# An ordering edge that keeps the products of the remaining modulation columns behind the first S5 projection on TensorE

## The chip, the core and the metric

The kernel runs on one core of a Trainium2 chip. The metric is the device time of one launch in microseconds, here the median of three runs. The program uses TensorE (matmuls), VectorE, ScalarE and GpSimd, and SyncE's queue for most of its loads and stores.

## What is computed: the reference

One layer of a diffusion backbone for 512 tokens of 1024 features, with 256 context tokens. In the reference, cut to what matters here:

```python
mod_x = (jax.nn.silu(c) @ w_ada[l] + b_ada[l])[:, None, :]
shx1, scx1, gx1, shx2, scx2, gx2 = jnp.split(mod_x, N_MOD, axis=-1)
px = modulate(rmsnorm(x, g_norm1[l]), shx1, scx1) @ w_in[l] + b_in[l]
pc = modulate(rmsnorm(ctx, g_norm1[l]), shc1, scc1) @ w_in[l] + b_in[l]
...
st_c = s5_states(uc, lam_bar, b_bar, None, dr == 1)
st_x = s5_states(ux, lam_bar, b_bar, h0, dr == 1)
y_x = y_x + s5_readout(st_x, s5_c_re[l, dr], s5_c_im[l, dr])
...
z_x = hyena_mixer(px[..., S5_W:], hy_conv_w[l], hy_conv_b[l], filt_x, hy_d[l], rows)
mix_x = merge_head_groups(y_x.reshape(B, L, S5_W), z_x, w_glu[l], b_glu[l],
...
x = x + gx1 * mix_x
hx2 = modulate(rmsnorm(x, g_norm2[l]), shx2, scx2)
x = x + gx2 * peer(hx2.reshape(B * L, D), peer_wq[l], peer_k1[l], peer_k2[l],
...
return rmsnorm(x, g_final)
```

The first projection `px` needs only the shift and the scale of the first norm (`shx1`, `scx1`), a third of the 6144 modulation columns. The other two thirds (`gx1`, `shx2`, `scx2`, `gx2`) are needed after the mixers.

## The kernel before

The front of the program, to about 476 us, computes everything up to the queries of the expert stage; behind it come the top-16 searches, the gathers and the two large products with the expert tables, which take the rest of the span. The names of the front are these.

- `pf`, `pke`, `pko`, `kk`: the Hyena filters and their spectra. A spectrum `kk` goes to the DRAM tile `KD` and comes back later as `sp`.
- `pmod`, `modr`: the first third of the modulation columns, and its transposes `modrT`, from which VectorE makes `mod` and `ax`.
- `pmodr`: the remaining columns, in two halves (`pmodr0`, `pmodr1`) of 8 steps each. A step is a call of `more_modulation`: for 128 rows of the weights two loads of 512 KB (`wb0_0_0`, `wb0_0_1`: half, step, side), and the products of each, which are four records in the trace. A "block" below is one such load with its products. The calls stand in `s5_context` and in the Hyena part, but their instructions carry a priority, so that the scheduler may draw them far forward.
- `xT0` to `xT7`: transposes of the normed input, eight blocks of 128 features. VectorE reads each out of PSUM (`xt`), and ScalarE and VectorE make the two parts `xs` (high and low) that a projection in three products needs. `cT`, `ct`, `cs` are the same for the context.
- `px0` to `px3`, `pc0` to `pc3`: the S5 part of the projection (24 matmuls each) of the tokens and of the context, with the weights `win0` to `win3`; `px4` to `px15` are the Hyena part. `px`, `pc`, `xT`, `cT` and the later `pu`, `pw` share a PSUM pool of two buffers.
- `wt1w`, `wt2w`, `et`, `E`, `ct13`, `Cr`, `ru`, `VP`, `H`: steps of the S5 scans on VectorE, in six groups; `edge`, `wt`, `pv` are their products on TensorE.
- `x2t`, `hq`: the short convolution of the Hyena part. `pu00` and `pw00` are the first products of its long convolution (with the table `fwd`), which VectorE multiplies with the spectrum in `spt000` to `spt003`.

The order in which this is written is the string `SEQ` (`M` makes `modrT`, `X` the `xT`, `U0` `px0`, `u0` `pc0`). The order in which each engine's queue holds it is made from that by a list scheduler with its own timeline, priorities and the edges that the program adds by hand (`add_manual_dep` with `NOSYNC`: it fixes an order on one engine, without a semaphore). Each engine, SyncE's queue included, then works in that order.

The weight loads share three buffers (`NRAW`, tag `wraw`): `win0r`, `win1r`, the `wb` and `win2r` onward take turns. A load is issued when the buffer's last reader is done.

Of the kernel before, what the change touches and what calls it, by code (L numbers as in the profile page):

```python
# [9 lines left out]
F32 = mybir.dt.float32  # L10
F32R = mybir.dt.float32r
# [62 lines left out]
SG = 32  # L74
# [35 lines left out]
NOSYNC = mybir.DependencyInfo(mybir.DependencyClass.NoSync, mybir.DependencyReason.DATA)  # L110
# [118 lines left out]
def build(tc, I, out, dbg=None, stop=None):  # L229
    nc = tc.nc  # L230
# [63 lines left out]
    def sm(name, shape, dtype=F32, bufs=1, tag=None):  # L294
        return cur[0].tile(shape, dtype, tag=tag or name, name=name, bufs=bufs)
# [80 lines left out]
    for what in EARLY.split():  # L376
        n = int(what[1:] or 0)
# [41 lines left out]
    sc = cp.tile([P, 8, 2], F32, tag="sc", name="sc")  # L419
# [200 lines left out]
        return s, c  # L620


    rest = [0, None]

    def more_modulation():
        with prio(PR_M):
# [2 lines left out]
    def more_modulation_():  # L629
        h_, k = rest[0] // 8, rest[0] % 8  # L630
        rest[0] += 1
        if k == 0:
            rest[1] = psn(f"pmodr{h_}")
            V.memset(rest[1], 0.0)
        pm = rest[1]
        for e in range(2):
            wa = wp.tile([P, D], F32, tag="wraw", name=f"wb{h_}_{k}_{e}", bufs=NRAW)
            c0 = 2048 * (h_ + 1) + D * e
            nc.sync.dma_start(wa, I["w_ada"][k * P:(k + 1) * P, c0:c0 + D])
            for n in (2 * e, 2 * e + 1):  # L640
# [39 lines left out]
    for part in SEQ.split():  # L680
        n_ = int(part[1:] or 0)
        if part[0] == "H":
            hid = feats
            for i in range(3):
                ph = ps5(f"ph{i}")[:, 0:256]
                n = 33 if i == 0 else 64
# [30 lines left out]
        elif part[0] == "S":  # L717
            t0, t1 = ((0, 4), None, (4, 6))[n_]
# [21 lines left out]
        elif part[0] == "P":  # L740
            k = n_
            if k == 0:
                pm = psm("pmod")
                V.memset(pm, 0.0)
            columns_of(pm, was[k], k, 2)
            if NWARM:
# [5 lines left out]
                for i in range(NWARM):  # L752
                    mm = PE.matmul(pwarm, warm[:, 0:P], warm, start=True, stop=True)
# [507 lines left out]
    for co in range(4):  # L1261
# [11 lines left out]
        t = g2_(f"cat5{co}", [P, 512])  # L1273
# [222 lines left out]
    def columns(lt, eid, gt):  # L1496

        ei = sm(f"ei{lt}", [P, 2, P], I32, tag="ei", bufs=2)
        V.tensor_copy(ei[:, 0], eid)
        V.tensor_scalar(ei[:, 1], ei[:, 0], 127, None, ALU.bitwise_and)  # L1500
        V.tensor_scalar(ei[:, 0], ei[:, 0], 7, None, ALU.logical_shift_right)
        ef = sm(f"ef{lt}", [P, 2, P], tag="ef", bufs=2)
        V.tensor_copy(ef, ei)
        ptr = ps.tile([P, 512], F32, tag="psc", name=f"ptr{lt}", bufs=2 if RGATE else 3)[:, 0:3 * P].rearrange("p (e n) -> p e n", e=3)
        PE.transpose(ptr[:, 0], ef[:, 0], ident)
        PE.transpose(ptr[:, 1], ef[:, 1], ident)
        PE.transpose(ptr[:, 2], gt, ident)
        if RGATE:
            t = sm(f"cols{lt}", [P, P], tag="cols", bufs=3)
            A.activation(t, ptr[:, 1], AF.Copy)  # L1510
            gh_ = sm(f"colg{lt}", [P, P], F32R, tag="colg", bufs=3)
            A.activation(gh_, ptr[:, 2], AF.Copy)
            V.tensor_tensor(ptr[:, 2], ptr[:, 2], gh_.bitcast(F32), ALU.subtract)
            return t, gh_.bitcast(F32), ptr
        t = sm(f"cols{lt}", [P, 5, P], tag="cols", bufs=3)
        A.activation(t[:, 0:3], ptr, AF.Copy)
        A.activation(t[:, 3:5], ptr[:, 0:3:2], AF.Copy, scale=-1.0)
        return t

    def gates_r(b_, cols, c0):  # L1520

        i2, gh_, ptr = cols
        st = sm(f"gst{b_}", [P, P, SG], tag="gst", bufs=2)

        def per_token(x, t0):
            return x[:, t0:t0 + 4].unsqueeze(2).broadcast_to((P, 4, P))

        for q in range(SG // 4):
            pg = ps.tile([P, 4, 2, P], F32, tag="pgg", name=f"pgg{b_}_{q}", bufs=2)
            t0 = c0 + 4 * q  # L1530
            o2 = sm(f"o2_{b_}_{q}", [P, 4, P], F32R, tag="o2", bufs=NOO)
            o1 = sm(f"o1_{b_}_{q}", [P, 4, P], tag="o1", bufs=NOO)
            os_ = sm(f"os{b_}_{q}", [P, 4, 2, P], F32R, tag="os", bufs=NOO)
            keys_ = iotak.unsqueeze(1).broadcast_to((P, 4, P))
            GP.tensor_tensor(o2, keys_, per_token(i2, t0), ALU.is_equal)
            V.tensor_tensor(o1, keys_, per_token(ptr[:, 0], t0), ALU.is_equal)
            V.tensor_tensor(os_[:, :, 1], o1, per_token(ptr[:, 2], t0), ALU.mult)
            for e in range(4):
                A.activation(os_[:, e, 0], o1[:, e], AF.Copy, scale=gh_[:, t0 + e:t0 + e + 1])
            for e in range(4):  # L1540
                mm = PE.matmul(pg[:, e].rearrange("p h i -> p (h i)"), o2[:, e], os_[:, e].rearrange("p h i -> p (h i)"), start=True, stop=True)
            groups.append(mm)
            so = st[:, :, 4 * q:4 * q + 4]
            A.activation(so, pg[:, :, 0].rearrange("p t i -> p i t"), AF.Copy)
            last = V.tensor_tensor(so, pg[:, :, 1].rearrange("p t i -> p i t"), so, ALU.add)
            gathers(G_SHARE, last)
            run_ahead(RG)
        nc.scalar.dma_start(GD[b_], st)
# [157 lines left out]
```

## Time and profile before

| | |
|---|---|
| median of three runs | 1786.19 us (1784.98 to 1787.14) |
| the profiled execution, its own time | 1782.07 us |
| its span, from the first to the last instruction | 1780.3 us |
| mean granted TensorE clock | 0.978 of full speed |
| busy, of the span | TensorE 1670.0 us (94%), VectorE 1491.0 us (84%), ScalarE 817.9 us (46%) |
| from 476 to 1778 us | TensorE busy 1264.76 of 1302 us |

All rows below come from the profiled execution, which was 4.1 us shorter than the median. Its span is 1.8 us shorter than its time. A row of a timeline gives the start in us from the span's start and the duration; a matmul's end overlaps its successor a little, so the starts tell the pace. `L441` is a line of the kernel before.

### The profile page before, as it was taken

To read this page: it belongs to the slowest core of one execution; us is meant where nothing else is said; L and a number is where in the kernel's file an instruction comes from. 1 tells how busy PE (TensorE), PEld (TensorE's weight loads), DVE (VectorE), ACT (ScalarE), POOL (GpSimd) and SP (SyncE) were. 2 spreads that over 40 slices of the span, in tenths; PEclk is the share of its full clock that TensorE was granted. 3 is DMA by queue.
4 is the path that set the end of the run, shared out by engine and by line. 5 is a ranking of instruction groups with operands and counts; after the bars stand their busy time and mean duration, and the time that the engine had idled before them with its cause. 6 is when DMAs were issued, how large, how long until landed. Compare 5 with 4: busy or idle time off the path is not lost.

```text
span 1780.3 us, 24942 instructions
## 1 busy us (share of the span) xinstructions
PE 1670.0 (94%) x8731; PEld 1410.6 (79%) x8731; DVE 1491.0 (84%) x3039; ACT 817.9 (46%) x1616; POOL 169.5 (10%) x158
## 2 busy tenths in 40 slices
PE   5799998789899999998999989999999999999997
PEld 1477654456799999998999978877878788999996
DVE  7965989986688989989999958788878787888887
ACT  3443543234433323236989844444434344444444
POOL 0000000000000000001101101111111112222221
PEclk9899999899899999999999989999999999999999
DMA  9436453122444444446989899999999998999981
GB/s 372 155 98 209 156 170 91 51 75 71 124 156 139 141 147 151 145 147 246 330 319 333 322 321 387 385 356 378 363 353 358 357 339 320 342 327 349 335 311 71
DMA packets 170228, 436.13 MB, mean 245 GB/s; under 512 B 17139, under 2 KB 102004, under 8 KB 150902
## 3 DMA queue, kind: packets, MB, share of 16 engines
q1 hardware_dynamic: 128854, 251.28, 41.8%
q0 software_dynamic: 18432, 134.23, 20.5%
q10 hardware_dynamic: 22816, 49.03, 7.6%
q8 instruction: 69, 1.13, 0.3%
q14 instruction: 57, 0.47, 0.1%
HBM read 381.52 MB, written 52.92 MB: 244 GB/s over the span
## 4 chain that ended last, share of the span: by engine, by line
PE 63%; DVE 12%; issue 1%; ACT 1%; DMA 1%; ACTq 0%; DVEq 0%
PE pacc L308 9%; PE pacc L309 9%; PE pacc L307 9%; PE pa L309 7%; PE pa L307 7%; PE pa L308 7%; PE pgg L1566 5%; PE pq L309 2%; PE pq L307 2%; PE pq L308 2%; DVE idx L1352 1%; DVE rs L1350 1%; PE pg L1266 1%; DVE idx L1348 1%; PE po L307 1%
## 5 line engine op out<-in xcount | busy, mean ns | idle before, releaser
L308 PE MATMUL pacc<-vl,wwh 128*128 128x512 f32 x768 | 299.6, 391 | 1.8 <-DVE vl L1607 1.8
L309 PE MATMUL pacc<-vh,wwl 128*128 128x512 f32 x768 | 295.1, 390 | 0.0
L1430 POOL DMA_INDIRECT uvr<-in_uv_dram,gidx x128 | 157.1, 1228 | 1090.6 <-DVE accg L1439 764.6
L307 PE MATMUL pacc<-vh,wwh 128*128 128x512 f32 x768 | 238.3, 391 | 8.4 <-ACT vh L1606 8.4
L1607 DVE TENSOR_TENSOR vl<-vr,vh 128x1024 fp32r<-128x1024 f32 x128 | 155.3, 1219 | 26.8 <-ACT vh L1606 26.7
L307 PEld LDWEIGHTS pacc<-vh,wwh 128*128 128x128 f32 x768 | 143.5, 188 | 39.4 <-ACT vh L1606 11.3
L308 PEld LDWEIGHTS pacc<-vl,wwh 128*128 128x128 f32 x768 | 144.1, 188 | 33.6 <-DVE vl L1607 3.6
L309 PEld LDWEIGHTS pacc<-vh,wwl 128*128 128x128 f32 x768 | 144.2, 188 | 29.7
L1439 DVE SCALAR_TENSOR_TENSOR accg<-uvr,wgt,accg 128x1024 f32<-128x1024 f32 x128 | 163.7, 1279 | 4.1 <-ACT wgt L1436 1.8
L1431 DVE SCALAR_TENSOR_TENSOR junk<-uvr,hrow 128x1024 f32<-128x1024 f32 x128 | 155.9, 1218 | 0.0
L1606 ACT ACTIVATE vh<-vr 128x1024 fp32r<-128x1024 f32 x128 | 133.0, 1050 | 44.1 <-PE pacc L309 33.8
L1615 ACT ACTIVATE wwh<-gw 128x384 fp32r<-128x384 f32 x128 | 67.1, 524 | 185.4 <-PE pacc L308 146.1
L1616 DVE TENSOR_TENSOR wwl<-gw,wwh 128x384 fp32r<-128x384 f32 x128 | 70.9, 554 | 53.9 <-ACT wwh L1615 53.9
L1566 PE MATMUL pgg<-o,o 128*128 128x128 f32 x768 | 93.0, 278 | 4.3 <-ACT o L1562 4.3
L1566 PEld LDWEIGHTS pgg<-o,o 128*128 128x128 f32 x768 | 92.1, 194 | 4.5 <-ACT o L1562 4.5
L1557 DVE TENSOR_TENSOR o<-iotak,cols 128x512 f32<-128x512 f32 x96 | 65.8, 685 | 10.1 <-PE pgg L1566 10.1
L1564 DVE TENSOR_SCALAR o<-iotak,cols 128x128 f32<-128x128 f32 x240 | 70.1, 342 | 0.0
L1434 ACT ACTIVATE wgt<-dots 128x1 f32<-128x1 f32 x128 | 25.3, 198 | 93.1 <-DVE junk L1431 93.1
L1562 ACT ACTIVATE o<-o,cols 128x128 f32<-128x128 f32 x144 | 63.6, 493 | 0.0
L1369 ACT ACTIVATE ga<-pa 128x384 f32<-128x384 f32 x128 | 60.4, 472 | 2.4 <-DVE gw L1612 2.1
L1568 ACT ACTIVATE gst<-pgg 128x512 f32<-128x512 f32 x96 | 56.7, 591 | 1.2 <-PE pgg L1566 1.1
L1612 DVE TENSOR_TENSOR gw<-gal,gc 128x384 f32<-128x384 f32 x88 | 48.4, 553 | 7.4 <-DMA gal<-GA 5.5
(1812 smaller groups left out, 4133.9 us busy)
## 6 DMA issues: line engine op xcount, KB each, us to landing
vr<-in_uv_dram SPq DMA_DIRECT2D x128, 512.0 KB
GD<-gst ACTq DMA_DIRECT2D x12, 2048.0 KB
gc<-GD SPq DMA_DIRECT2D x32, 768.0 KB
GA<-ga ACTq DMA_DIRECT2D x88, 192.0 KB
gal<-GA SPq DMA_DIRECT2D x88, 192.0 KB
wb<-in_w_ada_dram SPq DMA_DIRECT2D x32, 512.0 KB
wa<-in_w_ada_dram SPq DMA_DIRECT2D x8, 1024.0 KB
KD<-kk SPq DMA_DIRECT2D x16, 256.0 KB
```

What stands on the lines that cost most here:

```text
L307: nc.tensor.matmul(o, a[0], b[0], start=start, stop=False)
L308: nc.tensor.matmul(o, a[0], b[1], start=False, stop=False)
L309: nc.tensor.matmul(o, a[1], b[0], start=False, stop=stop_)
L1430: GP.indirect_dma_start(out=uvr, out_offset=None, in_=I["uv"], in_offset=bass.IndirectOffsetOnAxis(ap=gidx[:, s:s + 1], axis=0))
L1431: ins = V.scalar_tensor_tensor(junk, uvr[:, 0:D], 1.0, hrow, ALU.mult, ALU.mult, accum_out=dots[:, s:s + 1])
L1439: V.scalar_tensor_tensor(accg, uvr[:, D:2 * D], wgt[:, s:s + 1], accg, ALU.mult, ALU.add)
L1564: last = V.tensor_scalar(o1[:, e], iotak, cols[:, 0, t:t + 1], cols[:, 2, t:t + 1], ALU.is_equal, ALU.mult)
L1566: mm = PE.matmul(pg[:, e, :], o2[:, e], o1[:, e], start=True, stop=True)
L1606: A.activation(vh, vr, AF.Copy)
L1607: (V if QUIET or i >= P - VLV else GP).tensor_tensor(vl, vr, vh.bitcast(F32), ALU.subtract)
L1615: A.activation(wh, gw, AF.Copy)
L1616: last = V.tensor_tensor(wl, gw, wh.bitcast(F32), ALU.subtract)
```

## The change

A third entry of the list `rest` holds the name of the last instruction of `px0` once that is written. The next call of `more_modulation` then ties its first matmul to it by an edge without a semaphore, and clears the entry. All later products of `pmodr` follow that one. Before, nothing tied them. The other edits (the functions `columns` and `gates_r` and the loop that calls them) stand under `RGATE`, which is 0 in both programs, so that the built programs don't contain them; the diff shows the part that is built.

```diff
@@ -620,7 +620,7 @@
         return s, c
 
 
-    rest = [0, None]
+    rest = [0, None, None]
 
     def more_modulation():
         with prio(PR_M):
@@ -638,7 +638,10 @@
             c0 = 2048 * (h_ + 1) + D * e
             nc.sync.dma_start(wa, I["w_ada"][k * P:(k + 1) * P, c0:c0 + D])
             for n in (2 * e, 2 * e + 1):
-                PE.matmul(pm[32 * n:32 * n + 1], sc[:, k, 0:1], wa[:, (n % 2) * 512:(n % 2 + 1) * 512], start=k == 0, stop=k == 7, tile_position=(0, 32 * n))
+                mm = PE.matmul(pm[32 * n:32 * n + 1], sc[:, k, 0:1], wa[:, (n % 2) * 512:(n % 2 + 1) * 512], start=k == 0, stop=k == 7, tile_position=(0, 32 * n))
+                if rest[2] is not None:
+                    tc.add_manual_dep(mm.ins, rest[2], NOSYNC, reason="leaves the way to the first projections")
+                    rest[2] = None
         if k == 7:
             ptv = turned(pm, f"modr{h_}")
             for n in range(4):
@@ -657,6 +660,8 @@
         px = psa(f"px{ct}")
         for k in range(8):
             mm3(px, (wh[:, k, :], wl[:, k, :]), (xhi[k], xlo[k]), k == 0, k == 7)
+        if ct == 0:
+            rest[2] = nc.cur_bb.bb.instructions[-1].name
         if ct % 2 == 0:
             u2 = hy(f"uP{ct}", [P, 2, T8, NK])
         A.activation(u2[:, ct % 2, :, NKC:NK].rearrange("p j k -> p k j"), px.rearrange("p (k j) -> p k j", j=T8), AF.Identity, bias=b_in[:, ct:ct + 1])
@@ -1506,12 +1511,10 @@
```

The scheduler makes a new order of the whole front from it; from the queries of the expert stage on the rows are the same. Three places follow.

TensorE behind the transposes of the modulation rows (`modrT`), before:

```order
L434 MATMUL modrT_395<-ident_60,modr_393 128x98 x4
L641 MATMUL pmodr0_980<-wb0_0_0_982,sc_138 1x512 x2
L641 MATMUL pmodr0_980<-wb0_0_1_986,sc_138 1x512 x2
L641 MATMUL pmodr0_980<-wb0_1_0_1024,sc_138 1x512 x2
L641 MATMUL pmodr0_980<-wb0_1_1_1028,sc_138 1x512 x2
L441 MATMUL xT2_434<-ident_60,xrow0_99 128x128 x2
L441 MATMUL xT2_434<-ident_60,xrow2_100 128x128 x2
```

and after:

```order
L434 MATMUL modrT_395<-ident_60,modr_393 128x98 x4
L441 MATMUL xT2_434<-ident_60,xrow0_99 128x128 x2
L441 MATMUL xT2_434<-ident_60,xrow2_100 128x128 x2
L441 MATMUL xT3_443<-ident_60,xrow0_99 128x128 x2
L441 MATMUL xT3_443<-ident_60,xrow2_100 128x128 x2
L548 MATMUL rnc0_273<-ones_65,fsq010_324 128x1 x2
L576 MATMUL pke011_463<-hfb010_312,trig1_98 128x256 x4
```

The four blocks of `pmodr0` have gone from between `modrT` and `xT2`; three more have gone from between `xT3` and `xT7`.

TensorE from the last transposes to the first matmuls of `px0`, before:

```order
L441 MATMUL xT6_532<-ident_60,xrow2_100 128x128 x2
L641 MATMUL pmodr0_980<-wb0_3_0_1308,sc_138 1x512 x2
L441 MATMUL xT7_541<-ident_60,xrow0_99 128x128 x2
L441 MATMUL xT7_541<-ident_60,xrow2_100 128x128 x2
L576 MATMUL pke000_496<-hfb001_230,trig0_97 128x256 x4
L576 MATMUL pko000_497<-hfb001_230,trig0_97 128x256 x4
L576 MATMUL pke010_550<-hfb011_313,trig0_97 128x256 x4
L307 MATMUL px0_574<-xs0_412,win0h_570 128x512
```

after, up to the same point:

```order
L441 MATMUL xT6_532<-ident_60,xrow0_99 128x128 x2
L441 MATMUL xT6_532<-ident_60,xrow2_100 128x128 x2
L441 MATMUL xT7_541<-ident_60,xrow0_99 128x128 x2
L441 MATMUL xT7_541<-ident_60,xrow2_100 128x128 x2
L307 MATMUL px0_574<-xs0_412,win0h_570 128x512
```

and after, among and behind the last matmuls of `px0`:

```order
L576 MATMUL pke000_496<-hfb001_230,trig0_97 128x256 x4
L576 MATMUL pko000_497<-hfb001_230,trig0_97 128x256 x4
L576 MATMUL pke010_550<-hfb011_313,trig0_97 128x256 x4
...
L309 MATMUL px0_574<-xs1_413,win0l_571 128x512
L441 MATMUL cT0_602<-ident_60,crow4_101 128x128
L576 MATMUL pko010_551<-hfb011_313,trig0_97 128x256 x4
L441 MATMUL cT0_602<-ident_60,crow4_101 128x128
L641 MATMUL pmodr0_980<-wb0_0_0_982,sc_138 1x512 x2
L521 MATMUL pf200_633<-hwo1_96,hid2_187 128x256 x2
L521 MATMUL pf201_634<-hwo1_96,hid2_187 128x256 x2
L641 MATMUL pmodr0_980<-wb0_0_1_986,sc_138 1x512 x2
L441 MATMUL cT1_609<-ident_60,crow4_101 128x128 x2
```

The block `wb0_3_0` and the three filter groups `pke000`, `pko000` and `pke010` have gone from the way to `px0`; the three groups stand in `px0` now, in front of its last five matmuls, and the blocks of `pmodr0` begin behind it, among the filter products `pf` and the context transposes `cT`. Four blocks stand between `px0` and `px1` in the new order, where one stood before (`wb0_3_1`).

VectorE around the first product of the long convolution (`spt000`, at 280.99 us of the profile), before:

```order
L586 TENSOR_TENSOR ct13_2959<-PC0_870,cre_94 128x512
L586 TENSOR_TENSOR ct23_2960<-PC1_871,cre_94 128x512
L586 TENSOR_TENSOR wt1w5_2979<-PB0_868,bb_859 128x512
L586 TENSOR_TENSOR et4_3037<-EA0_880,EB1_883 128x384
L586 TENSOR_TENSOR et4_3037<-EA1_881,EB0_882 128x384
L586 TENSOR_TENSOR wt2w5_2980<-PB1_869,bb_859 128x512
L1128 SCALAR_TENSOR_TENSOR x2t_1674<-hp10_2239,small_91,x2t_1674 128x8x63
L1056 TENSOR_TENSOR wout11l_2642<-wout11r_2639,wout11h_2641 128x512
L586 TENSOR_TENSOR Cr3_2957<-ct13_2959,ct23_2960 128x512
L646 TENSOR_TENSOR mod_140<-modr1T_2298,small_91 128x4 x4
...
L586 TENSOR_TENSOR E4_3036<-et4_3037 128x384
L1163 TENSOR_TENSOR spt000_2323<-pu00_2317,sp00_2315 128x512
```

and after:

```order
L1132 SCALAR_TENSOR_TENSOR x2t_1674<-hp11_2283,small_91,x2t_1674 128x8x63
L586 TENSOR_TENSOR WBiw4_2869<-wt1w4_2870,wt2w4_2871 128x512
L1168 TENSOR_TENSOR spt000_2323<-pu00_2317,sp00_2315 128x512
L586 TENSOR_TENSOR ru03_2948<-ru03_2948,ru13_2949 128x256 x2
L586 TENSOR_TENSOR E4_3036<-et4_3037 128x384
L1169 TENSOR_TENSOR spt001_2324<-pw00_2318,sp00_2315 128x512
L1170 TENSOR_TENSOR spt002_2325<-pw00_2318,sp00_2315 128x512
L649 TENSOR_TENSOR mod_140<-modr1T_2298,small_91 128x4 x4
L1133 SCALAR_TENSOR_TENSOR x2t_1674<-hp11_2283,small_91,x2t_1674 128x8x63
L1171 TENSOR_TENSOR spt003_2326<-pu00_2317,sp00_2315 128x512
L586 TENSOR_TENSOR ct13_2959<-PC0_870,cre_94 128x512
L586 TENSOR_TENSOR ct23_2960<-PC1_871,cre_94 128x512
```

What stood ahead of `spt000` from `ct13` to `mod`, and the steps of `ru03` on 256 columns and of `E4` before them, stand behind it.

## Rows read from the trace of the kernel before

**Rows 1.** Busy by stretch: us, PE, PEld, DVE, ACT, POOL, clock, DMA, GB/s.

```profile
58.00:89.00 31.00, 21.08 (x109) 11.95 (x108) 29.87 (x69) 13.78 (x24) 0.00 (x0) 0.89 0.57 178
89.00:117.00 28.00, 26.20 (x120) 18.94 (x119) 17.10 (x34) 13.59 (x25) 0.00 (x0) 0.94 0.25 80
117.00:162.00 45.00, 44.63 (x252) 38.72 (x256) 19.87 (x35) 15.15 (x22) 0.00 (x0) 1.00 0.51 154
162.00:278.00 116.00, 110.19 (x638) 71.72 (x630) 106.26 (x182) 58.34 (x122) 1.95 (x10) 0.99 0.54 177
278.00:374.00 96.00, 75.00 (x355) 40.50 (x356) 94.18 (x165) 23.27 (x65) 1.23 (x6) 0.93 0.26 61
```

**Rows 2.** TensorE's timeline, 57 to 110 us: start, duration, idle before.

```profile
65.95 4.43 PE L641 MATMUL pmodr<-wb,sc 128*1 128x512 f32 x12 [6.64 <-DMA wb<-in_w_ada_dram]
70.31 1.25 PE L441 MATMUL xT<-ident,xrow 128*128 128x128 f32 x8
...
83.04 1.03 PE L641 MATMUL pmodr<-wb,sc 128*1 128x512 f32 x4 [1.67 <-DMA wb<-in_w_ada_dram]
...
84.49 1.89 PE L576 MATMUL pke<-hfb,trig 128*128 128x256 f32 x8
...
89.49 0.58 PE L307 MATMUL px<-xs,win0h 128*128 128x512 f32 x1
```

**Rows 3.** VectorE's waits, 57 to 89 us: total, times, longest in us.

```profile
DVE xt L445 <- ACT xs L443: 1.1, 2, 1.0
```

**Rows 4.** VectorE's timeline, 57 to 105 us.

```profile
67.31 1.51 DVE L445 TENSOR_SCALAR xt<-xT,ax,mod 128x512 f32<-128x512 f32 x2
...
83.67 0.79 DVE L445 TENSOR_SCALAR xt<-xT,ax,mod 128x512 f32<-128x512 f32 x1
```

**Rows 5.** Timeline of SyncE's DMA issues, 57 to 105 us.

```profile
61.52 3.39 SPq L639 DMA_DIRECT2D wb<-in_w_ada_dram  x3
...
76.89 1.26 SPq L639 DMA_DIRECT2D wb<-in_w_ada_dram  x1
```

**Rows 6.** TensorE's timeline: px1, the first pc0, and around pu00.

```profile
104.81 0.80 PE L307 MATMUL px<-xs,win1h 128*128 128x512 f32 x1 [0.60 <-DVE ct L445]
...
108.32 0.39 PE L309 MATMUL px<-xs,win1l 128*128 128x512 f32 x1
108.55 0.40 PE L307 MATMUL px<-xs,win1h 128*128 128x512 f32 x1
...
117.36 0.39 PE L307 MATMUL pc<-cs,win0h 128*128 128x256 f32 x1 [0.69 <-DVE ct L445]
...
276.13 0.42 PE L921 MATMUL edge<-WBiw,CM 128*32 128x128 f32 x8
...
278.97 1.98 PE L1161 MATMUL pu<-uw,fwd 128*128 128x512 f32 x4 [1.29 <-DMA fwd<-in_fwd_dram]
```

**Rows 7.** TensorE's waits, 117 to 278 us.

```profile
PE pmodr L641 <- DMA wb<-in_w_ada_dram: 4.8, 3, 3.1
```

**Rows 8.** Busy time of one stretch of the front, columns as above.

```profile
75.00:83.60 8.60, 5.32 (x39) 2.60 (x37) 8.44 (x21) 3.95 (x6) 0.00 (x0) 1.00 0.61 183
```

**Rows 9.** VectorE's timeline, 105 to 170 and 272 to 284 us.

```profile
125.43 1.21 DVE L303 TENSOR_TENSOR win2l<-win2r,win2h 128x1024 fp32r<-128x1024 f32 x1
...
162.24 0.69 DVE L586 TENSOR_TENSOR wt1w<-PB,bb 128x512 f32<-128x512 f32 x1 [4.27 <-DMA KD<-kk]
...
272.91 1.29 DVE L586 TENSOR_TENSOR ct<-PC,cre 128x512 f32<-128x512 f32 x2
...
276.26 0.74 DVE L1128 SCALAR_TENSOR_TENSOR x2t<-hp,small,x2t 128x504 f32<-128x504 f32 x1
...
278.40 0.73 DVE L1127 SCALAR_TENSOR_TENSOR x2t<-hp,small,x2t 128x504 f32<-128x504 f32 x1
...
280.99 0.69 DVE L1163 TENSOR_TENSOR spt<-pu,sp 128x512 f32<-128x512 f32 x1 [1.39 <-PE pu L1161]
```

**Rows 10.** VectorE's waits, 282 to 374 us.

```profile
DVE spt L1164 <- PE pw L1161: 0.4, 1, 0.4
```

More of the change, by code (lines that the diff above doesn't have):

```diff
@@ L1508, in columns @@
         if RGATE:
[L1509 to L1514, printed above, removed]
+            g = sm(f"colg{lt}", [P, 2, P], F32R, tag="colg", bufs=3)
+            A.activation(g[:, 0], ptr[:, 2], AF.Copy)
+            V.tensor_tensor(g[:, 1], ptr[:, 2], g[:, 0].bitcast(F32), ALU.subtract)
+            return ptr, g.bitcast(F32)
         t = sm(f"cols{lt}", [P, 5, P], tag="cols", bufs=3)
@@ L1520, in gates_r @@
     def gates_r(b_, cols, c0):
-        i2, gh_, ptr = cols
+        ptr, g = cols
         st = sm(f"gst{b_}", [P, P, SG], tag="gst", bufs=2)
-        def per_token(x, t0):
-            return x[:, t0:t0 + 4].unsqueeze(2).broadcast_to((P, 4, P))
         for q in range(SG // 4):
@@ L1530, in gates_r @@
             t0 = c0 + 4 * q
-            o2 = sm(f"o2_{b_}_{q}", [P, 4, P], F32R, tag="o2", bufs=NOO)
-            o1 = sm(f"o1_{b_}_{q}", [P, 4, P], tag="o1", bufs=NOO)
+            ts_ = slice(t0, t0 + 4)
+            oo = sm(f"oo{b_}_{q}", [P, 4, 2, P], F32R, tag="oo", bufs=NOO)
             os_ = sm(f"os{b_}_{q}", [P, 4, 2, P], F32R, tag="os", bufs=NOO)
[L1534 to L1537, printed above, removed]
+            V.tensor_tensor(oo, iotak.unsqueeze(1).unsqueeze(1).broadcast_to((P, 4, 2, P)),
+                            ptr[:, 0:2, ts_].rearrange("p e t -> p t e").unsqueeze(3).broadcast_to((P, 4, 2, P)), ALU.is_equal)
+            o1, o2 = oo[:, :, 0].bitcast(F32), oo[:, :, 1]
+            GP.tensor_tensor(os_[:, :, 1], o1, g[:, 1, ts_].unsqueeze(2).broadcast_to((P, 4, P)), ALU.mult)
             for e in range(4):
-                A.activation(os_[:, e, 0], o1[:, e], AF.Copy, scale=gh_[:, t0 + e:t0 + e + 1])
+                A.activation(os_[:, e, 0], o1[:, e], AF.Copy, scale=g[:, 0, t0 + e:t0 + e + 1])
             for e in range(4):
@@ L1580, in build @@
             nc.sync.dma_start(dbg["g"][lt * P:(lt + 1) * P], gts[:, lt])
-    cols = [columns(lt, eids[:, lt], gts[:, lt]) for lt in range(1, 4)]
+    if not RGATE:
+        cols = [columns(lt, eids[:, lt], gts[:, lt]) for lt in range(1, 4)]
     for lt in range(1, 4):
+        if RGATE:
+            cols_lt = columns(lt, eids[:, lt], gts[:, lt])
         for b_ in range(P // SG):
-            (gates_r if RGATE else gates)((lt - 1) * (P // SG) + b_, cols[lt - 1], b_ * SG)
+            (gates_r if RGATE else gates)((lt - 1) * (P // SG) + b_, cols_lt if RGATE else cols[lt - 1], b_ * SG)
     run_ahead(NRUN)
```

## The prediction

> **What bounds the kernel now.** I read the busy time by stretch first, because a share of the whole span says little of a change that only touches the first quarter: behind about 476 us the two programs issue the same instructions in the same order, so only the time at which that part starts can move. In front of it the bound changes hands [rows 1]. From 58 to 89 us, the stretch of the edit, VectorE is busy 29.87 of 31 us and TensorE 21.08. From 89 to 117 TensorE is the fuller one (26.20 of 28), from 117 to 162 it is full (44.63 of 45), and to 278 nearly so (110.19 of 116), with VectorE close to it (106.26). From 278 to 374 VectorE is the bound (94.18 of 96) and TensorE waits.
>
> Second, TensorE's timeline in the edited stretch. It stands still for 6.64 us before its second row of modulation products and for 1.67 us before its last one there, both times for a load of weights `wb` [rows 2]. Read alone, that looks like 8.3 us to win. Third, VectorE's waits in the same stretch: 1.1 us, all of them for ScalarE [rows 3]; none is for TensorE. Its timeline shows why TensorE's wait does no harm there. The transposes `xT0` and `xT1` fill the two PSUM buffers until VectorE reads them, which it does from 67.31 on, two reads in 1.51 us [rows 4]; `xT2` needs the first of these buffers. TensorE could not have gone on with `xT2` much before 68.1, whatever stood in its queue; it did at 70.31.
>
> **The change part by part.** The edits of the gate columns lie under a switch that is off, so they put nothing in the program and cost nothing. What is left is one ordering edge: no product of the remaining modulation columns may stand ahead of the last matmul of `px0` on TensorE. No arithmetic is added or removed.
>
> *Taken from the front.* Seven blocks of products (`wb0_0_0` to `wb0_3_0`) leave the place between `modrT` and `px0`. A block alone is 1.03 us and ends some 0.07 us under the next row (65.95 + 4.43 against 70.31), so 0.96 us in a stream [rows 2]; seven are 6.7 us. Two waits go with them. But the stretch has 31 - 21.08 = 9.9 us of idle TensorE, and its pace is VectorE's: each further `xT` waits for a read. What VectorE can win is its 1.1 us of waits. So the front gains about 1 us, not 8.3; 2.4 us if the conversions close up further behind it.
>
> *The start of `px0`.* It needs the buffer of `xT6`, which the read at 83.67 (0.79 us) frees [rows 4]; with VectorE 0.9 us ahead that is about 83.6, 5.9 us before today's 89.49 [rows 2]. The scheduler has also moved three groups of filter products (`pke000`, `pko000`, `pke010`) from before `px0` into it; today they lie between 84.49 and 89.49 [rows 2], 5.0 us. So 5.9 us earlier TensorE still has 6.7 + 5.0 = 11.7 us to do that lay behind it before: it is 5.8 us behind, at the point where it becomes the bound.
>
> *Up to `pc0`.* Four of the seven blocks now stand before `px1`, two more before the first `pc0`, and the seventh just ahead of `pc0`. Their loads share three buffers with `win2r` to `win4r`, and SP issues them in order. Today a load takes 4.4 us from issue (61.52) to product (65.95), and 6.1 from 76.89 to 83.04 [rows 2, 5]. The seventh block's buffer is freed only by the sixth block's product, some 3.2 us of work ahead, so I expect a new wait of 1.2 to 2.9 us, and take 1.9. `win2r` to `win4r` are queued on SP behind these loads. The first of them can go when the first block's product, behind `px0` near 98, has freed a buffer, and lands some 6 us later; VectorE makes `win2l` at 125.43 [rows 9], so some 20 us of cover remain. Without it VectorE, which works in order, would stand there with all that follows. Against the new wait stand 0.60 us before `px1` and 0.69 before `pc0`, waits for VectorE that a later TensorE swallows [rows 6]. 5.8 + 1.9 - 1.3 = 6.4 us late at `pc0`.
>
> *The clock.* `px1` ran its first eight matmuls at the lower of the clock's two levels (1.2 of 2.4 GHz), 3.51 us from 104.81 to 108.32, and then 0.23 us apart [rows 6]: 3.51 - 8 x 0.23 = 1.7 us lost, in a stretch with a mean granted clock of 0.94 [rows 1]. `px0` will start after a thinner stretch than today. Eight matmuls at the lower level would cost 1.7 us, all 24 of them 5.0 us. From 75 to 83.6, where TensorE is busy 5.32 of 8.6 us, the granted clock was 1.00 [rows 8], so I take nothing and keep 5.0 for the range. The Trainium skill ("TensorE: Matmul & The Clock Gate", the section "HAM oscillation — how this bites in real kernels") says that a kernel whose matmuls come in bursts with idle time between them falls back to half the clock and pays anew at each burst. By that rule the emptied stretch would cost up to those 5.0 us, and the sum below would be 10.0 instead of 5.0; the trace agrees for `px1`, not for the stretch at 75.
>
> *From `pc0` to `pu00`.* From 117 to 278 TensorE has 6.2 us of idle time [rows 1], 4.8 of it waits for later `wb` loads [rows 7], and then a wait of 1.29 us at `pu00` for the table `fwd`, which is fetched anyway [rows 6]. A later TensorE swallows such waits: I take half of the first, 3.1 us, and the whole of the second, between nothing and 7.5 in sum. The small products between 276.13 and that wait (`edge4`, `wt41`, `modr1T`) stand behind `pu00` in the new order: 278.97 - 1.29 - 276.13 = 1.5 us [rows 6]. 6.4 - 3.1 - 1.3 - 1.5 = 0.5 us late at `pu00`, between -2.6 and 4.9.
>
> *Behind `pu00`.* Today VectorE comes to `spt000` at 280.99 after a wait of 1.39 us for `pu00` [rows 9]. In the new order a string of S5 steps that stood ahead of `spt000` stands behind it (`ru03`, `E4`, `ct13` to `Cr3`, `mod`). From 272.91 to 279.60, where the wait begins, VectorE does little else: two `x2t` and one `wout11l` of about 0.65 us each [rows 9]. 6.69 less 1.9 is 4.8, and the pair of `ru03` halves and the first `E4`, further ahead, are an estimate of 1.1 more by the steps of 512 and 384 columns in these rows: 5.9 in sum. `spt000` can't start before `pu00` does, so VectorE stands for that time and does the work later, in a stretch where it waits 0.4 us in all [rows 10]. If TensorE were 6 us early at `pu00`, that would cover it; by the sum above it isn't. At the end of the stretch the last `sp` comes forward past 3.2 us of other work, of which I credit 1.0. Sum: 0.5 + 5.9 - 0.4 - 1.0 = 5.0 us.
>
> The profiled execution took 1782.07 us, 4.1 below the median of the runs (1786.19). 1782.1 + 5.0 = 1787.1 on its scale, 1791.2 on that of the median.
>
> **The rivals.**
>
> *Faster.* The waits of 8.3 us are on the path after all: `px0` and what S5 needs of it come 5.9 us earlier, and the blocks that follow fill gaps that exist anyway. For it: TensorE has 1.8 us of idle time from 89 to 117 and 6.2 from 117 to 278 [rows 1]. Against it: rows 3. It decides if the blocks find at least 8 us of gaps between `px0` and `pu00`; then the early start stays, and with the one late wait for `pu00` gone too the end moves by -5.9 - 1.4: about 1779.
>
> *No change.* The lag is absorbed. VectorE has 116 - 106.26 = 9.7 us of idle time from 162 to 278 [rows 1], and the first S5 step, `wt1w` at 162.24, waited 4.27 us for the spectra `KD` to leave [rows 9]; `pko100`, the last product these need, stands ahead of most of `pc3` now, so S5 may start when it does today. Then the time that VectorE gains in front of `spt000` isn't lost, because the moved steps fill waits that it has anyway. Against it: 5.0 us would have to fit in waits of which the greater part lies ahead of the moved steps. About 1786.
>
> *The lag in full.* Nothing is swallowed and the clock falls: 4.9 late at `pu00` by the upper bound, 4.5 behind it as above (5.9 - 0.4 - 1.0), half of the clock's 5.0, less the 1.1 that the front may give back: 10.8 us, about 1797.
>
> That the edge does nothing isn't a rival: the order shows the rows moved.
>
> **How the numbers follow.** 0.47 for the forecast (alone 1788.1 to 1795.6, by its bounds at `pu00`), 0.12 for the full lag, 0.19 for no change, 0.22 for faster. A measurement of this kernel tells about 0.2%, 3.6 us, from no change; of the forecast's own range the lowest part, 0.05, lies within that. So slower has 0.54, the same 0.24, faster 0.22. The range goes from 1780, which leaves out most of the faster case's lower half, to 1797.5, the middle of the full lag; some 0.2 is left out.
>
> **What would show it.** Right: behind `modrT` TensorE has a gap until about 68; VectorE's waits from 58 to 89 stay near 1 us; `px0` starts near 83.6, `px1` 1 to 2.5 us behind 104.81 and `pc0` about 6 behind 117.36; a wait for `wb` of 1 to 3 us stands ahead of `pc0`; `pu00` lies within 3.5 us of 278.97 and VectorE waits 4 us or more for it at `spt000`; the last `sp` and all that follows is 4 to 7 us late. Wrong: a `px0` before 80, or a `px1` not behind 104.81, takes the lag away; a wait of under 2 us at `spt000` with S5 starting by 162 makes it the second rival; a stretch behind `spt000` as long as today's would say that the moved steps cost nothing, which is the step I am least sure of.

## The result and the profile after

The changed kernel took 1796.41 us (median of 6 runs, 1793.95 to 1799.45) against 1786.66 for the kernel before (6 runs, 1784.25 to 1789.53): a ratio of 1.0053, 95% interval 1.0042 to 1.0065, so 9.75 us slower. The forecast was 1791.2, with 1797.5 as the upper end of its range. The profiled execution took 1797.08 us with a span of 1795.3. Against the 1782.07 of before that is 15.0 us, more than the medians show: before's profiled execution lies 4.6 us under its median, this one 0.7 over its own. A difference between the two traces is thus up to 5 us larger than the one between the medians, and a second trace of the new order (e12 below) stands 12.9 us behind before's, at the point from which the rows are the same, where the first stands 14.1.

The busy time by stretch, in the columns of [rows 1]:

```profile
58.00:89.00 31.00, 17.91 (x78) 14.72 (x79) 28.59 (x62) 12.86 (x23) 0.00 (x0) 0.72 0.19 60
89.00:117.00 28.00, 28.00 (x129) 17.01 (x127) 16.24 (x31) 13.10 (x23) 0.00 (x0) 1.00 0.40 132
117.00:162.00 45.00, 42.99 (x227) 35.53 (x228) 18.53 (x35) 14.63 (x22) 0.00 (x0) 0.92 0.53 167
162.00:278.00 116.00, 112.04 (x663) 75.90 (x661) 101.73 (x172) 57.31 (x118) 2.03 (x10) 1.00 0.56 188
278.00:374.00 96.00, 73.50 (x348) 38.95 (x348) 89.47 (x158) 26.34 (x70) 1.25 (x6) 0.89 0.21 55
```

From 58 to 89 TensorE is busy 17.9 us where it was busy 21.1, and its granted clock fell from 0.89 to 0.72. From 89 to 117 it has no idle time left (28.00 of 28). VectorE's busy time from 278 to 374 fell from 94.18 to 89.47. TensorE's timeline answers to [rows 2, 6]:

```profile
67.22 1.97 PE L441 MATMUL xT<-ident,xrow 128*128 128x128 f32 x8 [9.81 <-DVE xt L445]
...
82.66 0.79 PE L307 MATMUL px<-xs,win0h 128*128 128x512 f32 x1 [1.48 <-DVE xt L445]
83.25 0.63 PE L308 MATMUL px<-xs,win0h 128*128 128x512 f32 x1
...
85.93 0.40 PE L309 MATMUL px<-xs,win0l 128*128 128x512 f32 x1
...
96.84 1.03 PE L641 MATMUL pmodr<-wb,sc 128*1 128x512 f32 x4
...
105.84 0.48 PE L307 MATMUL px<-xs,win1h 128*128 128x512 f32 x1
...
121.07 1.87 PE L641 MATMUL pmodr<-wb,sc 128*1 128x512 f32 x4 [2.01 <-DMA wb<-in_w_ada_dram]
122.87 0.58 PE L307 MATMUL pc<-cs,win0h 128*128 128x256 f32 x1
123.25 0.41 PE L308 MATMUL pc<-cs,win0h 128*128 128x256 f32 x1
...
284.11 3.37 PE L1166 MATMUL pu<-uw,fwd 128*128 128x512 f32 x4 [6.94 <-DMA fwd<-in_fwd_dram]
```

The gap in front of the transposes is no longer for `wb`: TensorE waits 9.81 us for VectorE's read, as [rows 4] had it. `px0` starts 6.8 us earlier, `px1` 1.0 us later, `pc0` 5.5 us later, behind a new wait of 2.01 us for the seventh block's load. At `pu00` a wait of 6.94 us for `fwd` stands where 1.29 stood. VectorE has no wait from 57 to 89 us; its list there, 1.1 us before [rows 3], is empty. Its timeline, which answers to [rows 4, 9]:

```profile
66.37 1.51 DVE L445 TENSOR_SCALAR xt<-xT,ax,mod 128x512 f32<-128x512 f32 x2
...
81.81 0.79 DVE L445 TENSOR_SCALAR xt<-xT,ax,mod 128x512 f32<-128x512 f32 x1
...
168.47 0.69 DVE L586 TENSOR_TENSOR wt1w<-PB,bb 128x512 f32<-128x512 f32 x1 [2.01 <-DMA KD<-kk]
...
287.52 0.69 DVE L1168 TENSOR_TENSOR spt<-pu,sp 128x512 f32<-128x512 f32 x1 [6.53 <-PE pu L1166]
...
386.40 1.29 DVE L586 TENSOR_TENSOR ru<-H,E 128x512 f32<-128x512 f32 x2
```

S5 starts 6.2 us late (168.47 against 162.24), `spt000` 6.5. The last row is the S5 step that reads the last `H`, 12.2 us later than before, where it was this row:

```profile
374.24 1.28 DVE L586 TENSOR_TENSOR ru<-H,E 128x512 f32<-128x512 f32 x2
```

So 5.6 us more are lost between `spt000` and that step, where VectorE has no other wait. Its list of waits for 282 to 388 us has one row:

```profile
DVE spt L1168 <- PE pu L1166: 6.5, 1, 6.5
```

And SP's issues, which answer to [rows 5]:

```profile
60.58 3.41 SPq L639 DMA_DIRECT2D wb<-in_w_ada_dram  x2
...
116.60 0.38 SPq L639 DMA_DIRECT2D wb<-in_w_ada_dram  x1
...
267.81 0.33 SPq L639 DMA_DIRECT2D wb<-in_w_ada_dram  x1
269.43 0.33 SPq L1057 DMA_DIRECT2D wout10r<-in_w_out_dram  x1
269.86 0.37 SPq L1057 DMA_DIRECT2D wout11r<-in_w_out_dram  x1
272.50 0.33 SPq L1155 DMA_DIRECT2D fwd<-in_fwd_dram  x1
```

The load for the block at 121.07 is issued at 116.60, behind the product that frees its buffer (115.13 to 116.09). `fwd` is issued 0.8 us earlier than before, right behind a `wb` and two `wout` loads, and is used 11.6 us later where 5.7 were enough. Before it was this row:

```profile
273.28 0.33 SPq L1150 DMA_DIRECT2D fwd<-in_fwd_dram  x1
```

### The profile page after: what moved, and what is told of

It is laid out like the page before. It is cut to its first block, busy times and chain, and to the rows that moved or that the text cites. A ratio compares the mean times of both kernels' runs of the same rounds, so it can differ in the third digit from the quotient of the medians.

```text
span 1795.3 us, 24953 instructions
## 1 busy us (share of the span) xinstructions
PE 1673.2 (93%) x8731; PEld 1415.3 (79%) x8731; DVE 1491.4 (83%) x3039; ACT 818.8 (46%) x1616; POOL 167.9 (9%) x158
## 4 chain that ended last, share of the span: by engine, by line
PE 62%; DVE 11%; issue 1%; DMA 1%; ACT 1%; DVEq 0%; ACTq 0%; SPq 0%
PE pacc L308 9%; PE pacc L309 9%; PE pacc L307 9%; PE pa L309 7%; PE pa L307 7%; PE pa L308 7%; PE pgg L1565 5%; PE pq L309 2%; PE pq L307 2%; PE pq L308 2%; DVE idx L1357 1%; DVE rs L1355 1%; PE pg L1271 1%; DVE idx L1353 1%; DVE val L1352 1%
## 5 line engine op out<-in xcount | busy, mean ns | idle before, releaser
L307 PEld LDWEIGHTS pacc<-vh,wwh 128*128 128x128 f32 x768 | 143.4, 188 | 39.4 <-ACT vh L1608 11.3
L1556 DVE TENSOR_TENSOR o<-iotak,cols 128x512 f32<-128x512 f32 x96 | 65.7, 684 | 10.3 <-PE pgg L1565 10.3
```

## The experiments

Twelve kernels ran, four at a time on one chip with the kernel before between them (its medians there: 1784.09, 1783.84 and 1784.52). One table first, since all are read in the same way: how much later than in before's trace (first row, in us) each point starts. "S5 end" is the step that reads the last `H`, "Y end" the last `py`, "rhr" the point behind which all kernels issue the same. The last columns are the difference of the medians and the ratio with its interval. Each row of points is one execution. That of e11, whose front is before's, and that of e9 from `pc0` on lie within 1.6 us of before's everywhere, so a smaller difference between two traces says little.

| run | px0 | pc0 | px5 | wt1w | pu00 | spt000 | S5 end | Y end | rhr | median | ratio |
|---|---|---|---|---|---|---|---|---|---|---|---|
| before | 89.5 | 117.4 | 162.6 | 162.2 | 279.0 | 281.0 | 374.2 | 382.7 | 473.5 | | |
| after | -6.8 | +5.5 | +8.0 | +6.2 | +5.1 | +6.5 | +12.2 | +14.3 | +14.1 | +9.8 | 1.0053 [1.0042, 1.0065] |
| e12 | -5.8 | +6.9 | +9.7 | +6.8 | +4.0 | +5.8 | +12.9 | +13.2 | +12.9 | +11.4 | 1.0059 [1.0040, 1.0079] |
| e1 | -5.7 | +7.2 | +10.0 | +11.4 | +9.8 | +11.2 | +11.5 | +12.9 | +12.9 | +11.0 | 1.0060 [1.0042, 1.0078] |
| e2 | -1.2 | +0.1 | +2.5 | +4.1 | -0.4 | +1.4 | +8.0 | +8.1 | +8.6 | +6.8 | 1.0039 [1.0025, 1.0053] |
| e3 | -6.3 | +6.5 | +9.2 | +8.4 | +8.2 | +8.2 | +8.5 | +8.5 | +8.5 | +6.6 | 1.0039 [1.0022, 1.0056] |
| e4 | -0.4 | -0.4 | -0.4 | -0.3 | -2.2 | -2.2 | +3.4 | +5.2 | +6.2 | +4.2 | 1.0019 [1.0008, 1.0031] |
| e5 | -1.4 | -2.7 | -1.4 | -0.8 | +2.9 | +4.7 | +4.7 | +7.3 | +6.6 | +1.2 | 1.0012 [0.9997, 1.0027] |
| e6 | -6.6 | +3.4 | +5.8 | +3.8 | -0.4 | +1.4 | +8.2 | +8.3 | +8.3 | +7.3 | 1.0046 [1.0028, 1.0064] |
| e7 | -5.6 | +7.0 | +8.6 | +5.6 | +1.1 | +1.1 | +8.0 | +8.0 | +7.3 | +6.1 | 1.0038 [1.0024, 1.0051] |
| e8 | +0.9 | -0.4 | +0.8 | +0.7 | -7.8 | -7.9 | -8.1 | +1.1 | +11.3 | +9.0 | 1.0048 [1.0030, 1.0066] |
| e9 | -6.0 | -0.9 | -0.9 | -0.5 | -1.3 | -1.3 | -1.3 | -1.3 | -0.9 | -0.6 | 0.9998 [0.9984, 1.0012] |
| e10 | +0.9 | +7.2 | +8.7 | +10.3 | +9.5 | +9.5 | +9.9 | +9.9 | +9.9 | +10.5 | 1.0055 [1.0035, 1.0074] |
| e11 | +0.4 | +0.4 | +0.4 | +0.3 | -1.1 | -1.1 | -1.1 | +1.5 | +1.0 | -1.1 | 0.9999 [0.9984, 1.0013] |

The scheduler answers one edge with a new order in many places, so the diff alone can't be cut into parts. All kernels but e8 therefore have the order of every engine and queue written down, and the parts are exchanged in that list:

```diff
+def keep_order(tc):
+    import base64, json, zlib
+    nc = tc.nc
+    traced = {i.name: i for i in nc.cur_bb.bb.instructions}
+    at, last = 0, {}
+    for step in json.loads(zlib.decompress(base64.b85decode(ORDER))):
+        at += step
+        i = traced.get(f"I-{at}")
+        if i is None:
+            continue
+        if i.engine in last:
+            tc.add_manual_dep(i, last[i.engine], NOSYNC, reason="keeps a written order")
+        last[i.engine] = i.name
...
+        keep_order(tc)
```

**Where on the way is it lost?** Four hybrids: the changed kernel's order up to the first matmul of `px4` and before's from there (e1), the reverse (e2), and both again with the seam at `px14` (e3, e4). Nothing else differs.

> Every engine and queue works in the changed kernel's order up to the first matmul of px4, and behind it in the order of the kernel before. Theory A (the time is lost around the first spectra: the table fwd comes late and S5 steps stand behind spt000): the lag of about 10 us that TensorE shows at px4 is swallowed by px14, as in the changed kernel's trace, and the time is that of the kernel before, 1785 to 1789 us. Theory B (the time is lost in the front: TensorE's lag at px0 to px4 and the S5 start, 6 us late, carry to the end): 1793 to 1798 us.

> The reverse: the order of the kernel before up to the first matmul of px4, so that the modulation products stay in the front, and the changed kernel's order behind it. Theory A: 1792 to 1797 us, nearly the whole loss, with a wait for fwd or a late spt000 and the last H over 5 us behind. Theory B: 1785 to 1788 us.

> The changed kernel's order up to the first matmul of px14, the order of the kernel before behind it, so that ct13 to Cr3 stand ahead of spt000 again. Theory A with the S5 steps as its main part: 1786 to 1790 us. Theory A with the late fwd as its main part: 1791 to 1796, since the loads of the weights ahead of it come as late as in the changed kernel. Theory B, or a loss between px4 and px14: 1793 to 1798.

> The order of the kernel before up to the first matmul of px14, the changed kernel's behind it. Theory A with the S5 steps as its main part: 1791 to 1795 us, with a wait before spt000 of 4 us and more. Theory A with the late fwd: 1786 to 1789, since the loads ahead of fwd come as early as before. Theory B: 1785 to 1788.

The new front by itself (e1) costs 11.0 us, and its lag of 10.0 at `px5` arrives at the end almost unchanged: before's order swallows nothing of it on balance. With the seam at `px14` (e3) the new front is 8.2 us late at `spt000` and 8.5 at the end of the trace, 6.6 by the medians. The new order behind `px4` by itself (e2) costs 6.8 us, with `spt000` only 1.4 us late; behind `px14` by itself (e4) it costs 4.2, with `spt000` even 2.2 us early. In both, 5.6 to 6.6 us are lost between `spt000` and the end of S5, as in the changed kernel (5.6, and 7.1 in e12, where VectorE also waits 1.3 us there) and unlike in e1 and e3 (0.3). That is the string of S5 steps behind `spt000`: in the changed kernel, e2 and e4 VectorE's rows between the two points differ from before's in these steps alone, which take 5.8 us by their starts. The costs don't add: 11.0 + 6.8 would be 17.8, and the change cost 9.75. Where the new order from `px4` on is in force, TensorE wins back 7.3 us between `px5` and the last matmul of `px15` in e2 and 8.8 in the changed kernel. Three things make it, by the starts in the changed kernel's timeline. 4.8 us of waits for `wb` [rows 7] are gone, with 2.7 us of waits for `win9` and `win10` in their place. Small products of S5 and `modr1T`, 1.7 us, now stand outside the stretch. And the same 22 blocks take 14.9 us between `px5` and `pu00` and not 18.5: more of them stand next to each other, and two such blocks, which write different strips of PSUM (`tile_position=(0, 32 * n)`), take hardly more than one. A block alone, before, and two next to each other, after:

```profile
185.17 1.03 PE L641 MATMUL pmodr<-wb,sc 128*1 128x512 f32 x4
```

```profile
230.31 1.04 PE L641 MATMUL pmodr<-wb,sc 128*1 128x512 f32 x8
```

The three come to 7.4 of the 8.5 us by which TensorE moves forward between `px5` and its wait at `pu00`.

e2 also shows the late `fwd`, without any lag ahead of it:

```profile
278.61 3.78 PE L1161 MATMUL pu<-uw,fwd 128*128 128x512 f32 x4 [5.40 <-DMA fwd<-in_fwd_dram]
```

**Did the waits in the front cost anything, and did the blocks?** e5 is before's order and e6 the changed kernel's, both without the seven blocks.

```diff
+            if h_ == 0 and 2 * k + e < 7:
+                continue
...
-                PE.matmul(pm[32 * n:32 * n + 1], ..., start=k == 0, ...)
+                PE.matmul(pm[32 * n:32 * n + 1], ..., start=k == (0 if h_ else 4 - e), ...)
```

> The kernel before in its own order, without the seven blocks wb0_0_0 to wb0_3_0: their seven loads and their products are left out, so that this half of the modulation sums is incomplete. If those blocks lie in the shadow of VectorE in the front, as the prediction has it, the time hardly falls: 0 to 2 us less than before. If the 8.3 us of waits that TensorE shows there are on the path, it falls by 6 us or more.

> The changed kernel in its own order without the same seven blocks (the same part of the modulation sums is left out). If the lag of TensorE at px4 is their work behind px0, the wait for wb0_3_0 and the half clock at pc0, px4 comes at or ahead of the time of the kernel before, and the loss shrinks to that of the order behind px4, which alone made 6.8 us. If the lag comes from the filter groups or from something else in the front, px4 stays 5 us late or more, and the time within 3 us of the changed kernel's.

e5 gains nothing (+1.2 us, the interval includes none): seven blocks of products and 8.3 us of waits taken out of the front are worth `px0` 1.4 us earlier. TensorE's waits from 57 to 89 us in e5:

```profile
PE xT L441 <- DVE xt L445: 10.1, 2, 9.8
PE rnr L562 <- ACT norm L557: 1.6, 1, 1.6
PE pke L576 <- DVE hfb L566: 1.5, 1, 1.5
```

The time that TensorE spent on the blocks and on waits for `wb` has become a wait for VectorE. Its +6.6 in the table is one execution's late `fwd` (a wait of 5.72 us at `pu00`, with before's order of loads), which the median doesn't show.

e6 was meant to take the lag away, and left 5.8 us at `px5`. Three filter groups (5.0 us) are behind the early `px0` still, and an emptier TensorE had the lower clock in more places: the granted clock was 0.67 from 58 to 89 us and 0.88 from 89 to 117, and `px0`, `px1` and `pc0` each began at the lower clock:

```profile
82.89 0.80 PE L307 MATMUL px<-xs,win0h 128*128 128x512 f32 x1 [1.47 <-DVE xt L445]
83.49 0.63 PE L308 MATMUL px<-xs,win0h 128*128 128x512 f32 x1
...
106.94 0.63 PE L308 MATMUL px<-xs,win1h 128*128 128x512 f32 x1
...
120.99 0.41 PE L308 MATMUL pc<-cs,win0h 128*128 128x256 f32 x1
```

By the starts, from `px0` to `px5`, `px0`, `px1` and the first `pc0` take 3.7 us longer than before's, the waits for VectorE are 2.1 us longer, and the filter products `pf` take 1.8 us longer in their new order. So the work of the blocks isn't all of the lag: a good part stays when they are not done at all.

**Blocks or filter groups?** The change moves both. e9 takes before's order and moves only filter groups, the three that stand ahead of `px0` from 84.49 on into it and a fourth from within it to behind it; e10 takes e1's order and puts the three groups back ahead of `px0`, so that of the two only the blocks have moved. (`pko010`, and the order of `pf`, `cT` and some of VectorE's steps, stay as in the new front.)

> The kernel before in its own order, but the filter groups pke000, pko000 and pke010 stand behind the 19th matmul of px0 and pko010 behind its last, as in the changed order; the modulation blocks stay in the front. By the count of work this only permutes TensorE: px0 starts 5 us earlier and ends at the same time, px4 0 to 2 us late, the time within 2 us of before. If the spectra kk that VectorE makes from these groups come late and hold what follows in its order (ct, hfb, then pf and px1), px4 is 3 us late or more and the time 3 to 7 us longer.

> The order of e1 (the changed kernel's up to px4, that of before behind it, 11 us slower than before), but the three filter groups go back ahead of px0: only the seven blocks are moved. By the count of work px0 starts near 86 and 3.4 us of the lag stay, with the wait for wb0_3_0 and its clock 5 to 8 us at px4, and the time is 4 to 8 us over before. If the groups are what costs, the lag at px4 is under 3 us and the time within 3 us of before. If the order of the groups doesn't matter at all, it is e1's 11 us.

e9 is no change (0.9998): `px0` comes 6.0 us earlier and nothing else comes more than 1.4 us earlier. e10 has the whole loss, 10.5 us, with the groups back in their place, and loses it even though `px0` isn't any earlier. Its busy times from 58 to 89 us, and TensorE's timeline:

```profile
58.00:89.00 31.00, 18.41 (x73) 15.06 (x74) 27.86 (x58) 12.71 (x22) 0.00 (x0) 0.62 0.19 60
```

```profile
66.47 1.97 PE L441 MATMUL xT<-ident,xrow 128*128 128x128 f32 x8 [9.81 <-DVE xt L445]
...
82.27 3.78 PE L576 MATMUL pke<-hfb,trig 128*128 128x256 f32 x8 [1.80 <-DVE hfb L566]
85.84 3.18 PE L576 MATMUL pko<-hfb,trig 128*128 128x256 f32 x8
88.86 1.89 PE L576 MATMUL pke<-hfb,trig 128*128 128x256 f32 x8
90.39 0.58 PE L307 MATMUL px<-xs,win0h 128*128 128x512 f32 x1
...
122.75 1.87 PE L641 MATMUL pmodr<-wb,sc 128*1 128x512 f32 x4 [2.43 <-DMA wb<-in_w_ada_dram]
```

The granted clock of the front was 0.62, and two filter groups took 3.78 and 3.18 us where 1.89 is the price at full clock [rows 2]: what the start of `px0` had to win went there. In e9, which keeps the blocks, `px0` begins almost at full clock:

```profile
83.51 0.50 PE L307 MATMUL px<-xs,win0h 128*128 128x512 f32 x1
83.84 0.39 PE L308 MATMUL px<-xs,win0h 128*128 128x512 f32 x1
```

Why e10's lag then stays whole is in its waits. TensorE's from 117 to 290 us, and SP's from 117 to 290 us, first in e10 and then before:

```profile
PE pmodr L641 <- DMA wb<-in_w_ada_dram: 6.2, 3, 3.0
```

```profile
SPq L639 <- PE pmodr L641: 43.6, 13, 9.0
```

```profile
SPq L639 <- PE pmodr L641: 43.6, 12, 9.1
```

Later products found their weights hardly sooner: the three waits for `wb` are 6.2 us, the new one ahead of `pc0` (2.43) among them, against 4.8. So 1.0 us of before's waits went (1.7 in e1), and a new wait of 1.5 us (1.3 in e1) for VectorE's `WBiw` took its place. SP issues these loads when a product has freed a buffer, so a late TensorE makes its own loads late.

**Is the late `fwd` its place in the queue?** e7 is the changed kernel's order with the loads `wout10r` and `wout11r` behind `fwd` and `inv` on SP, and their four conversions later. e11 is before's order with the eight loads of `KT0`, issued in the same stretch, moved behind `inv` (on SP) and behind `VS4` (on ACT).

> The changed kernel in its own order, but the loads wout10r and wout11r go behind those of fwd and inv on SyncE's queue, and their two conversions on ScalarE and two on VectorE behind the steps of the second spectrum. If fwd comes late at pu00 because these 512 KB stand ahead of it in the queue, the 6.9 us wait for it shrinks to 1 to 3 us and the time by 3 to 5 us. If the transfers of KT that start with it hold fwd, the wait stays over 5 us and the time the same.

> The kernel before in its own order, but the eight loads of KT0, which is read from 333 us on, go behind the issue of inv on SyncE's queue and behind VS4 on ScalarE's. If they hold fwd, the wait for it at pu00 is gone in every execution, the spread of the times shrinks, and the median falls by 1 to 4 us, so that this beats both kernels. If the wait is set by what stands ahead of fwd, nothing changes within 1 us.

> The changed kernel again, the same instructions in the same order, for a second trace beside the others of this chip: 8 to 11 us over before, with a wait for fwd at pu00 of 5 us or more if that belongs to its order, and of 1 to 7 if it is chance.

In e7 `pu00` waits 1.42 us and runs at full clock:

```profile
280.10 1.98 PE L1166 MATMUL pu<-uw,fwd 128*128 128x512 f32 x4 [1.42 <-DMA fwd<-in_fwd_dram]
```

`spt000` is 1.1 us late and not 6.5, and the time 6.1 us over before where the change had 9.75 and, in its second measurement (e12), 11.4. So 3.6 to 5.2 us go with that wait; the intervals of the ratios overlap, so the size is not sure. e12 shows the wait again, 4.49 us. e11's wait is 0.44 us, and neither its time (0.9999) nor its spread (1779.83 to 1788.78) gains: the 1.29 us of before are no loss that shows.

**Can the columns of the second half wait instead?** e8 leaves the first half where it was and issues the blocks of the second half later, behind the spectra of `S = 0`; the scheduler orders the rest.

```diff
-            more_modulation()
+            if ct < 4:
+                more_modulation()
...
+                if o == 0:
+                    more_modulation()
+                    more_modulation()
```

> The kernel before with the eight calls for the second half of the remaining modulation columns written into the loop of the first spectra, behind pu00, where TensorE waits for VectorE (ah is made behind them too), and the scheduler free. If TensorE's 15 us of these products and its 4.8 us of waits for their loads hold the stretch from 162 to 278 us, the time falls by 3 to 8 us. If VectorE is the real bound of that stretch, it stays within 2 us of before, or rises with the loads that then meet fwd.

`pu00` and the end of S5 came 8 us earlier, and it lost 9.0 us all the same: the last `sp` of Hyena starts at 386.40 where it was 373.63, and the point behind which all is alike 11.3 us late. The scheduler has put Hyena's chain behind the S5 steps that came forward. I did not take that order apart.

## Why the prediction held, and where it was off

**The front** was right. VectorE sets its pace, 8.3 us of TensorE's waits for `wb` were harmless (e5), and `px0` came at 82.66 where 83.6 was forecast. The rival that counted on these waits ("faster") is refuted by e5 and e9. The one that had the lag absorbed ("no change") fails at S5, which starts 6.2 us late.

**The lag** was right in its main parts: seven blocks and three filter groups behind an earlier `px0`, a wait of 2.01 us ahead of `pc0` where 1.9 was taken, 5.5 us late at `pc0` where 6.4 was. That the sum came so near is in part luck: `pf` took 1.4 us more in its new order, which no term had, and `px1` 1.5 us less. e9 and e10 correct the reading: the groups are an exchange of places, and moving the blocks, from a stretch where TensorE has time to one where it has none, is enough for the whole cost. How much of that is their work and how much the clock and the small changes of order that e10 keeps is not taken apart; e6 shows that it isn't their work alone.

**The clock** was mis-sized: taken at nothing, with 5.0 us kept for the range. The window at 75 to 83.6 that had a clock of 1.00 [rows 8] contained the blocks that the change takes away. Measured: the first six matmuls of `px0` came 0.43 us apart and not 0.23 (1.2 us), the block ahead of `pc0` took 1.87 and not 1.03 (0.8), and the first sixteen of `pc0` came 0.21 apart and not 0.12 (1.5): 3.5 us. The 1.7 us that `px1` lost before were not lost here, so 1.8 us net by the end of `pc0`. The Trainium skill ("TensorE: Matmul & The Clock Gate", the section "HAM oscillation — how this bites in real kernels") has matmuls in bursts with idle time between them pay the lower clock anew at each burst. The trace agrees at the transposes behind 9.81 us of idle time (1.97 us where 1.25 stood), at `px0`, ahead of `pc0` and at `pu00`; the 5.0 us that I had worked out by it is more than the 3.5 found.

**From `pc0` to `pu00`** the forecast of 0.5 us late was 4.6 off. Half of the waits for `wb` were to be swallowed by the lag. In before's order 1.7 (e1) and 1.0 us (e10) are, and new waits for VectorE take their place; the longest, 3.1 us, stays (3.13 and 3.04), because the loads hang on TensorE's products. In the changed kernel they vanish with the new places of the products, and the pairs of blocks save 3.6 us, which no term had. With all this TensorE was ready for `pu00` 0.5 us earlier than before (284.11 - 6.94 against 278.97 - 1.29). What was missed is `fwd`: a wait of 1.29 us was credited as swallowed, and it grew to 6.94. Its load was put down as "fetched anyway", and no row was read for what stands ahead of it on SP. `pu00` then ran at the lower clock, 3.37 us and not 1.98.

**Behind `pu00`** the step that I was least sure of held: 5.9 less 0.4 was forecast for the moved S5 steps, and 5.6 measured, 5.6 to 6.6 in e2 and e4 where they are alone with the new tail. The credit of 1.0 us at the end of the stretch was wrong. The last `sp` did come forward (8.3 us late, the S5 step 12.2), but nothing behind it gained: the last `py` is 2.1 us later still. That is the clock once more, in this execution: the products `pk` ahead of it, behind waits of 1.67 and 0.46 us, had a granted clock of 0.54 and took 3.53 us, where 1.92 stood before:

```profile
392.55 3.53 PE L1044 MATMUL pk<-KT,Ur 128*64 128x128 f32 x32 [0.46 <-DMA KT<-FT]
```

In e12 they took 1.97 us, and the last `py` is only 0.3 us later than the S5 step.

In sum, on the traces' scale: 6.53 at `spt000`, 5.63 from there to the end of S5, 2.13 to the last `py`, 0.72 behind it, 15.01 in all where 5.0 was forecast. The medians differ by 9.75. The lag in full (1797) came nearest in size, but not on its path: it had no late `fwd`, and what it had not swallowed was won back ahead of `pu00`.

So the mechanism was right up to `pc0` and for the S5 steps, and the forecast had half of the loss. That 1796.41 lies in the range, 1.1 us under its upper end, is partly luck, since that end was set by the full lag. Of the signs, those up to `pc0` came, and the wait of 4 us or more at `spt000` (6.53). `pu00` was 5.1 us late and not within 3.5, and the last `sp` and what follows 8.3 to 14 us and not 4 to 7.

**Left open.** How much of the late `fwd` is its place and how much is chance: with a `wb` and two `wout` loads just ahead it made `pu00` wait 6.94, 4.49, 5.40 and 5.39 us (after, e12, e2, e6), in before's order of these loads mostly 0.4 to 1.8 us (before, e1, e9, e10, e11), and 5.72 once (e5). A buffer of its own for `fwd` was not tried. Nor was e10's order without the blocks, which would part their work from the clock. No kernel here beats the one before; e9 and e11 equal it.

## What to carry to other kernels

Work that lies in another engine's stretch is free there, even if its own waits look like the loss; an edge that pushes it to where its own engine is full cost more than its length here, since the engine also fell to the lower clock in the stretch it left. Waits for loads whose buffers are freed by the same engine's work absorbed little of the lag (1.0 to 1.7 of 4.8 us), since they move along with it. When a scheduler answers one edge with another order everywhere, write the orders down and exchange them piece by piece: here the new front cost 11.0 us, the new tail 6.8, and both together 9.75.

## What the runs showed of the hardware

- TensorE's granted clock depended on work that was worth nothing by itself. From 58 to 89 us it was 0.89 with the seven blocks there (before, e9) and 0.62 to 0.78 without them (e10, e6, after and e5).
- Two blocks of `pmodr` next to each other, on different strips of PSUM, took 1.04 us where one took 1.03 (after, before).
- The first products behind a long wait at `pu00` ran at the lower clock: 3.37 to 3.78 us behind waits of 4.49 to 6.94, against 1.95 to 1.99 behind 0.44 to 1.71. One does not fit: 3.34 behind 1.83 (e1).
- A load issued behind others in one queue had no fixed price: `fwd` was used 4.8 to 11.6 us after its issue (e11, after), and 5.7 or 10.1 with the same three kinds of load ahead of it (before, e5).
